# Token scales in two pieces, a gate's scaling behind the next low part, and more projection ahead of the second inverse

## The chip, the core and the metric

The kernel runs on one core of a Trainium2 chip. The metric is the device time of one execution in microseconds. Five engines matter here. TensorE (PE in the profile, PEld for its weight loads) multiplies, VectorE (DVE) and ScalarE (ACT) work elementwise and empty the accumulation banks, GpSimd (POOL) works elementwise between buffers of the on-chip memory, and SyncE (SP) issues the transfers.

## The reference, cut to what matters

One layer of a hybrid encoder over 16 meta tokens and 512 real ones, model width 2048:

```python
hn = rmsnorm(h_res, norm_in_g)
P = hn @ w_in                       # 2048 -> 8320 columns
# RWKV-7 half: token shift, then r, k, v, g (1024 wide each), low-rank inputs wl, al
decay = exp(-exp(-softplus(-(w0 + tanh(wl) @ w_lora_up)) - 0.5))
a = sigmoid(a0 + al @ a_lora_up)
kk = k * k_k / norm(k * k_k);  k = k * (1 + (a - 1) * k_a)
y = recurrence(r, decay, k, v, kk, kk * a)   # 16 heads of 64, delta rule
y_a = (groupnorm(y) + bonus) * silu(g)
# convolution half: B, C, h, g_c (1024 wide each)
y_b = B * causal_conv3(C * h) * silu(g_c)
h_res = h_res + concat(y_a, y_b) @ w_out
out = rmsnorm(h_res)[16:]
```

## The kernel before, in words

**Products.** Everything is kept transposed, channels on the partitions. The input projection is cut into 65 column tiles of 128 (`plan`: first the low-rank tile lora, then k0, r0, B0, v0, k1 and so on; k, r, v, g belong to the RWKV half, C, h, B, gc to the convolution half). Both operands are split into a high and a low part, and a product of a 128x128 block is three products: high by high, high by low x, low weight by high x (`steps`, line 328 is the matmul). A column tile with 528 or 514 tokens takes 96 matmuls in two banks, one with 512 tokens (B, gc) takes 48 in one bank.

**Weights.** `prefetch` (from line 138) issues one transfer of 128x1024 on SP and splits it into two quarters of 128x512: ACT casts the high part (line 134), DVE or POOL subtracts to get the low part (line 135). Six quarters fit (`slot`, six buffers). DVE makes the low part of the first quarter of each transfer, POOL that of the second. The dictionary `low` holds the low part's instruction of each quarter.

**Token scales.** The normalisation is not applied to the input. Its factor per token, `rs`, multiplies each projection as it leaves its bank (`scaled`, line 352). The factor is made once, in `token_scale_sums` and `token_scale`: five small matmuls sum the squares of 128 tokens each (line 459), DVE divides and adds (line 463), POOL raises the eight columns to the power -1/2 in one instruction (`rsqrt`, line 98) and copies five of them out to 128 columns each (`yb`, line 468). TensorE transposes each, so that the factor of a token lies on all partitions (lines 475 and 478), and DVE copies the result into `rs` (lines 476 and 479).

**The first four tiles.** lora, k0, r0 and B0 go side by side, a quarter of each at a time (`mains`). In the last round, the sums stand after k0, four transposes stand between r0's first bank and its second, the fifth stands in the middle of B0.

**Stages.** Pairs of heads are prepared two at a time (`prepare`), and `invert` inverts their triangular matrices together. The first call, for 0 and 1, is the first inverse; the call for 2 and 3 is the second. In `invert`, two 32x32-block transposes per pair member on DVE (`xn`, line 843) feed small matmuls on TensorE (`t`, line 852: 32 for the first member, then 32 for the second). Between such steps, `fill(ns)` lets projection matmuls through, each counted at 0.43 ns a column (220 ns for 512 columns), until the given time is used. `FW["solve_first"]` is 30,000 and `FW["solve"]` 24,500 for the later three. The projection's order does not change by that, only what stands between its matmuls. After an inverse, `prepare` asks for the next k tile to be complete (`until`).

**Order.** TensorE's order is written out by hand: it is the order of the program. The queues of DVE, ACT and POOL are put in an order by a planner that works with its own estimates of time; weights and some steps are given a higher priority. `issue_after(x)` adds that an instruction on x's engine stands behind x in that queue. `behind_of("split")` uses it: lines 521 and 522 store for B tiles 1 to 3 the first low part of the next tile, and `use` puts the scaling of the B tile behind it (line 436). For the gate tiles gc the scaling has no such tie. An engine's queue is worked off in order, so whatever stands ahead of an instruction has to be done first.

Of the kernel before, what the change touches and what calls it, by code (L numbers as in the profile page):

```python
# [18 lines left out]
P = 128  # L19
# [3 lines left out]
META = 16  # L23
# [54 lines left out]
def hymba_kernel(ctx: ExitStack, tc: tile.TileContext, xt, xtok, front, w_in, w_out, pv, lup, cst, msk, gf, out):  # L78
    nc = tc.nc
# [17 lines left out]
    def rsqrt(y, v):  # L97
        nc.gpsimd.tensor_tensor(out=y, in0=v, in1=mhalf[:, 0 : v.shape[1]], op=ALU.pow)
# [217 lines left out]
    REAL = ((0, SEQ),)  # L316
    PLACED = ((0, SEQ, META), (SEQ, SEQ + 2, META - 2), (SEQ + 2, L, 0))

    def steps(ps, ranges, k4, q, ks=range(4), rs_=range(2)):
        hi, lo = quarters[q]  # L320
        for r, (a, b) in enumerate(ranges):
            if r not in rs_:
                continue
            for k in ks:
                kt = 4 * k4 + k
                w = slice(k * P, (k + 1) * P)
                for n, (ww, xx) in enumerate(((hi, xh), (hi, xl), (lo, xh))):
                    nc.tensor.matmul(  # L328
                        ps[r], ww[:, w], xx[:, kt, a:b], start=(kt == 0 and n == 0), stop=(kt == KT - 1 and n == 2)
                    )  # L330
                    yield (b - a) * 0.43
# [14 lines left out]
    def scaled(ranges, ps, dst, base):  # L346
        for (a, b), p in zip(ranges, ps):
            for c, d, t in PLACED:
                c0, d0 = max(a, c), min(b, d)
                if c0 < d0:  # L350
                    o = t + c0 - c - base
                    nc.vector.tensor_tensor(
                        out=dst[:, o : o + d0 - c0], in0=p[:, c0 - a : d0 - a], in1=rs[:, c0:d0], op=ALU.mult
                    )
# [42 lines left out]
    def behind_of(what):  # L397
        return tc.issue_after(state.pop(what)) if what in state else nullcontext()

    def use(what, i, ps):  # L400
        if what == "lora":
            use_lora(ps)
        elif what in ("k", "v"):
            t = cq.tile([P, LP], F32, tag=what, name=f"{what}{i}")
            nc.gpsimd.memset(t[:, META:CH], 0.0)
            shift_full(ps, tile_of[what] + i, f"{what}{i}", padded(t))
            got[what, i] = t
        elif what in ("r", "g"):
            t = cq.tile([P, SEQ], F32, tag=f"r{i % 2}" if what == "r" else "g", name=f"{what}{i}")
            shift_real(ps, tile_of[what] + i, f"{what}{i}", t)  # L410
            if what == "g":
                gate(t, f"r{i}")
                later(14000, lambda: nc.sync.dma_start(gated[i], t))
            got[what, i] = t
        elif what == "C":
            u = tm(f"u{i}")
            scaled(TAIL, ps, u, 14)
            got[what, i] = u
        elif what == "h":
            u = got["C", i]  # L420
            hh = tm(f"hh{i}")
            with behind_of("turned"):
                scaled(TAIL, ps, hh, 14)
            n = SEQ + 2
            nc.gpsimd.tensor_tensor(out=u[:, 0:n], in0=u[:, 0:n], in1=hh[:, 0:n], op=ALU.mult)
            cv = tp.tile([P, SEQ], F32, tag="cw", name=f"cv{i}")
            nc.scalar.activation(cv, u[:, 0:SEQ], AF.Copy, scale=col(V_CW, i))
            for j in (1, 2):
                nc.vector.scalar_tensor_tensor(
                    out=cv, in0=u[:, j : j + SEQ], scalar=col(V_CW, 8 * j + i), in1=cv, op0=ALU.mult, op1=ALU.add  # L430
                )
            got[what, i] = cv
            if i == 0:
                nc.gpsimd.tensor_tensor(out=cv, in0=cv, in1=got["B", 0], op=ALU.mult)
        elif what == "B":
            b = tm(f"b{i}")[:, 0:SEQ] if i else cq.tile([P, SEQ], F32, name="b0")
            with behind_of("split"):
                scaled(REAL, ps, b, META)
            got[what, i] = b
            if i:  # L440
                nc.gpsimd.tensor_tensor(out=got["h", i], in0=got["h", i], in1=b, op=ALU.mult)
        else:
            cv = got["h", i]
            g = tm(f"gc{i}")[:, 0:SEQ]
            scaled(REAL, ps, g, META)
            gate(g, f"c{i}")
            o = direct.get(8 + i, cv)
            nc.vector.scalar_tensor_tensor(out=o, in0=cv, scalar=0.5, in1=g, op0=ALU.mult, op1=ALU.mult)
            if o is cv:
                later(9000, lambda: nc.sync.dma_start(mixd[8 + i], cv))  # L450
        ready.add((what, i))
# [4 lines left out]
    def token_scale_sums():  # L456
        pss = pi.tile([P, 8], F32, tag="misc", name="pss")
        for j, (a, b) in enumerate(((0, 128), (128, 256), (256, 384), (384, 512), (512, L))):
            nc.tensor.matmul(pss[0 : b - a, j : j + 1], accd[:, a:b], cs[:, C_ON : C_ON + 1], start=True, stop=True)
        var = tp.tile([P, 3, 8], F32, tag="nv", name="var0")  # L460
        nc.gpsimd.memset(var[:, 0], 1.0)
        for a, b, n in ((0, 4, P), (4, 5, META)):
            nc.vector.tensor_scalar(
                out=var[:n, 0, a:b], in0=pss[:n, a:b], scalar1=1.0 / DM, scalar2=RMS_EPS, op0=ALU.mult, op1=ALU.add
            )
        rsqrt(var[:, 1], var[:, 0])
        yb = cq.tile([P, 5, P], F32, tag="gt0", name="yb")
        nc.gpsimd.tensor_copy(yb, var[:, 1, 0:5].unsqueeze(2).to_broadcast([P, 5, P]))
        return yb

    def token_scale(yb, part):
        prs = pi.tile([P, 512], F32, tag="misc", name="prs")
        if part == 0:
            for j in range(4):
                nc.tensor.transpose(prs[:, j * P : (j + 1) * P], yb[:, j], ident)
            nc.vector.tensor_copy(rs[:, 0:512], prs)
        else:
            nc.tensor.transpose(prs[:, 0:META], yb[0:META, 4], ident[0:META, 0:META])
            nc.vector.tensor_copy(rs[:, 512:L], prs[:, 0:META])

    def mains():
        pa = banks(FULL, "lora", pm, "main")
        pb = banks(FULL, "k0", pz, "tz")
        pc = banks(TAIL, "r0", pm, "main")
        pd = [pi.tile([P, SEQ], F32, tag="ser", name="ps_B0")]
        four = ((pa, FULL), (pb, FULL), (pc, TAIL), (pd, REAL))
        for k in range(4):
            for n, (ps, rg) in enumerate(four):
                if k == n == 0:
                    hi, lo = quarters[0]  # L490
                    for ww, xx, first in ((hi, xh, True), (lo, xh, False), (hi, xl, False)):
                        for p, (a, b) in zip(ps, rg):
                            nc.tensor.matmul(p, ww[:, 0:P], xx[:, 0, a:b], start=first, stop=False)
                            yield (b - a) * 0.43
                    continue
                yield from steps(ps, rg, 0, 2 * n, (k,))
        for k4 in range(1, 4):
            for n, (ps, rg) in enumerate(four):
                h = 4 * (k4 // 2) + n
                if k4 == 2:  # L500
                    prefetch(h + 3)
                if (k4, n) == (3, 2):
                    yb = token_scale_sums()
                if (k4, n) == (3, 3):
                    yield from steps(ps, rg, k4, 2 * h + k4 % 2, range(2))
                    token_scale(yb, 4)
                    use("lora", 0, pa)
                    use("k", 0, pb)
                    yield from steps(ps, rg, k4, 2 * h + k4 % 2, range(2, 4))
                    continue  # L510
                for r in range(2 if n < 3 else 1):
                    if (k4, n, r) == (3, 2, 1):
                        token_scale(yb, 0)
                    yield from steps(ps, rg, k4, 2 * h + k4 % 2, range(4), (r,))
        use("r", 0, pc)
        use("B", 0, pd)
        for j in range(4, len(plan)):
            what, i = plan[j]
            rg = FULL if what in ("k", "v") else REAL if what in ("B", "gc") else TAIL
            ps = yield from main(j, rg, f"{what}{i}")  # L520
            if what == "B" and i < 4:
                state["split"] = low[4 * j + 4]
            use(what, i, ps)

# [305 lines left out]
    def invert(two):  # L830
        first = two[0]["i"]
        both = range(2)
        fill(FW["solve"] if first else FW["solve_first"])
        run_pending(float("inf"))


# [680 lines left out]
```

## Time and profile before

| what | value |
|---|---|
| median of 3 runs | 1017.98 us (1017.09 to 1019.04) |
| the profiled execution | 1016.83 us, its span 1015.1 us |
| granted TensorE clock over that span | 0.998 |
| PE busy | 995.6 us, 98% |
| DVE busy | 684.3 us, 67% |
| ACT busy | 393.9 us, 39% |
| POOL busy | 276.2 us, 27% |

A row of the timeline gives start and duration in us, the engine, the line of the kernel, the operation, the tiles written and read, their shapes and how many instructions were merged into the row; in brackets stands how long the engine was idle before it and what ended that. The list of waits has, for each instruction and releaser, the total in us, how often, and the longest.

### The profile page before, as it was taken

The numbers are of one execution on the slowest core, as the hardware profiler recorded it, in microseconds if no ns is written. First come the engines' busy times: TensorE is split into PE (matmuls) and PEld (weight loads), VectorE is DVE, ScalarE is ACT, GpSimd is POOL, SyncE is SP. The second block draws the span as 40 slices with busy tenths as digits, with TensorE's granted clock in tenths as the row PEclk, the third lists the DMA queues.
The fourth block names the chain that finished last, engine by engine and source line by source line (L and its number), as shares of the span: only waits on it lengthen the run. The fifth ranks groups of instructions, "written<-read, shape, count | busy, mean of one in ns | idle before, by whom it ended". The sixth has DMA issues, their size and how long they took to land.

```text
span 1015.1 us, 23761 instructions
## 1 busy us (share of the span) xinstructions
PE 995.6 (98%) x9723; PEld 913.6 (90%) x9723; DVE 684.3 (67%) x1305; ACT 393.9 (39%) x729; POOL 276.2 (27%) x292
## 2 busy tenths in 40 slices
PE   9999999999999999999999999999999999999996
PEld 8899998999988999998999998889898897787875
DVE  7677955587775568654668654244555697998787
ACT  7553423344323433323434323222222335545453
POOL 0122323233232323222423222223332332015001
PEclk9999999999999999999999999999999999999999
DMA  9525576446664363864273956977673698696754
GB/s 325 158 75 140 127 193 172 120 119 149 160 167 134 100 176 87 220 166 118 83 172 95 222 140 188 342 241 229 220 211 88 196 264 190 171 330 139 174 124 166
DMA packets 185037, 174.83 MB, mean 172 GB/s; under 512 B 121568, under 2 KB 142816, under 8 KB 184416
## 3 DMA queue, kind: packets, MB, share of 16 engines
q1 hardware_dynamic: 182336, 164.40, 56.3%
q0 software_dynamic: 2304, 8.39, 5.0%
q8 instruction: 76, 1.25, 0.5%
q10 hardware_dynamic: 288, 0.52, 0.1%
q14 instruction: 33, 0.27, 0.1%
HBM read 136.92 MB, written 36.35 MB: 171 GB/s over the span
## 4 chain that ended last, share of the span: by engine, by line
PE 55%; DVE 8%; DMA 3%; issue 2%; ACT 1%; SPq 0%; POOL 0%; DVEq 0%; ACTq 0%; POOLq 0%
PE ps_gc L328 8%; PE ps_B L328 7%; PE ps_h L328 7%; PE ps_C L328 6%; PE ps_v L328 5%; PE ps_k L328 5%; PE ps_g L328 4%; PE ps_r L328 4%; DVE o L1213 3%; DMA wo<-in_w_out_dram 2%; PE M L1240 2%; PE zy L1009 1%; PE zs L1005 1%; PE g L680 1%; DVE xb L1221 1%
## 5 line engine op out<-in xcount | busy, mean ns | idle before, releaser
L134 ACT CAST w<-wr 128x512 fp32r<-128x512 f32 x252 | 153.2, 618 | 292.7 <-PE ps_k L328 45.8
L135 POOL TENSOR_TENSOR w<-wr,w 128x512 fp32r<-128x512 f32 x119 | 166.6, 1400 | 362.0 <-ACT w L134 310.6
L135 DVE TENSOR_TENSOR w<-wr,w 128x512 fp32r<-128x512 f32 x133 | 94.3, 715 | 104.7 <-ACT w L134 99.6
L328 PE MATMUL ps_k<-xh,w 128*128 128x256 f32 (+1 forms) x512 | 95.6, 284 | 1.1 <-DVE w L135 1.1
L328 PE MATMUL ps_r<-xh,w 128*128 128x256 f32 (+1 forms) x512 | 95.7, 282 | 0.0
L328 PE MATMUL ps_v<-xh,w 128*128 128x272 f32 (+1 forms) x512 | 95.1, 283 | 0.0
L328 PE MATMUL ps_h<-xh,w 128*128 128x258 f32 (+1 forms) x512 | 94.1, 282 | 0.0
L328 PE MATMUL ps_C<-xh,w 128*128 128x258 f32 (+1 forms) x512 | 93.2, 281 | 0.0
L328 PE MATMUL ps_g<-xh,w 128*128 128x258 f32 (+1 forms) x512 | 92.2, 281 | 0.0
L328 PE MATMUL ps_B<-xh,w 128*128 128x512 f32 x256 | 83.4, 394 | 0.0
L328 PEld LDWEIGHTS ps_k<-xh,w 128*128 128x128 f32 x512 | 80.5, 190 | 1.6 <-DVE w L135 1.4
L328 PE MATMUL ps_gc<-xh,w 128*128 128x512 f32 x256 | 81.4, 393 | 0.3 <-DVE w L135 0.3
L328 PEld LDWEIGHTS ps_r<-xh,w 128*128 128x128 f32 x512 | 80.5, 189 | 0.2
L328 PEld LDWEIGHTS ps_h<-xh,w 128*128 128x128 f32 x512 | 79.7, 189 | 0.7
L328 PEld LDWEIGHTS ps_v<-xh,w 128*128 128x128 f32 x512 | 80.1, 189 | 0.3
L328 PEld LDWEIGHTS ps_C<-xh,w 128*128 128x128 f32 x512 | 79.6, 189 | 0.6
L328 PEld LDWEIGHTS ps_g<-xh,w 128*128 128x128 f32 x512 | 79.4, 189 | 0.5
L328 PE MATMUL ps_k<-xl,w 128*128 128x272 f32 (+1 forms) x256 | 73.1, 286 | 0.0
L328 PE MATMUL ps_h<-xl,w 128*128 128x256 f32 (+1 forms) x256 | 72.0, 281 | 0.6 <-issue 0.6
L328 PE MATMUL ps_v<-xl,w 128*128 128x256 f32 (+1 forms) x256 | 72.5, 283 | 0.0
L328 PE MATMUL ps_r<-xl,w 128*128 128x256 f32 (+1 forms) x256 | 72.3, 282 | 0.0
L328 PE MATMUL ps_g<-xl,w 128*128 128x256 f32 (+1 forms) x256 | 72.2, 282 | 0.0
(321 smaller groups left out, 2278.0 us busy)
## 6 DMA issues: line engine op xcount, KB each, us to landing
wr<-in_w_in_dram SPq DMA_DIRECT2D x126, 512.0 KB
ct<-opd SPq DMA_DIRECT2D x64, 288.0 KB
wo<-in_w_out_dram SPq DMA_DIRECT2D x24, 512.0 KB
x<-in_w_out_dram POOLq DMA_DIRECT2D x16, 512.0 KB, 6.2
opd<-ar SPq DMA_DIRECT2D x8, 576.0 KB
opd<-gt SPq DMA_DIRECT2D x16, 288.0 KB
opd<-bt SPq DMA_DIRECT2D x64, 64.0 KB
x<-in_w_out_dram SPq DMA_DIRECT2D x8, 512.0 KB
```

What stands on the lines that cost most here:

```text
L134: nc.scalar.copy(hi, rq)
L135: low[q] = eng.tensor_tensor(out=lo, in0=rq, in1=hi.bitcast(F32), op=ALU.subtract).ins
L328: nc.tensor.matmul(ps[r], ww[:, w], xx[:, kt, a:b], start=(kt == 0 and n == 0), stop=(kt == KT - 1 and n == 2))
L680: nc.tensor.matmul(z[h][:, c - c0], bk[hs, c, h : h + 2, :].rearrange("p a s -> p (a s)"), ar[hs, c].rearrange("p a s -> p (a s)"), start= ...
L1005: nc.tensor.matmul(d[hs, j], w, x[hs], start=(a == 0), stop=(a == b - 1))
L1009: nc.tensor.matmul(d[ho, j], t[hs, o : o + CH], x[hs], start=(a == 0), stop=(a == b - 1))
L1213: nc.vector.tensor_tensor(out=lo, in0=rq, in1=hi.bitcast(F32), op=ALU.subtract)
L1221: nc.vector.tensor_tensor(out=h, in0=h, in1=ps, op=op)
L1240: nc.tensor.matmul(bank[s], left(prod, jj, m, s), w, start=(jj == 0 and n == 0), stop=(jj == 7 and n == 2))
```

## The change

Four edits in three places.

- The power is taken in two instructions, columns 0 to 3 and then column 4, each followed by its own copy into `yb`. Before, it was one power over eight columns and one copy of five.
- The four transposes are moved from between r0's two banks to behind r0's second bank, ahead of B0's last quarter. The fifth stays in the middle of that quarter.
- The scaling of gate tile gc0 is tied behind the first low part of the tile that follows it (k2).
- `fill` ahead of the second inverse gets 2,400 ns more, 26,900 in place of 24,500. The other inverses keep theirs.

```diff
         else:
             cv = got["h", i]
             g = tm(f"gc{i}")[:, 0:SEQ]
-            scaled(REAL, ps, g, META)
+            with behind_of("split"):
+                scaled(REAL, ps, g, META)
             gate(g, f"c{i}")
...
-        rsqrt(var[:, 1], var[:, 0])
         yb = cq.tile([P, 5, P], F32, tag="gt0", name="yb")
-        nc.gpsimd.tensor_copy(yb, var[:, 1, 0:5].unsqueeze(2).to_broadcast([P, 5, P]))
+        for a, b in ((0, 4), (4, 5)):
+            rsqrt(var[:, 1, a:b], var[:, 0, a:b])
+            nc.gpsimd.tensor_copy(yb[:, a:b], var[:, 1, a:b].unsqueeze(2).to_broadcast([P, b - a, P]))
         return yb
...
                 if (k4, n) == (3, 3):
+                    token_scale(yb, 0)
                     yield from steps(ps, rg, k4, 2 * h + k4 % 2, range(2))
                     token_scale(yb, 4)
...
                 for r in range(2 if n < 3 else 1):
-                    if (k4, n, r) == (3, 2, 1):
-                        token_scale(yb, 0)
                     yield from steps(ps, rg, k4, 2 * h + k4 % 2, range(4), (r,))
...
-            if what == "B" and i < 4:
+            if what == "B" and i < 4 or (what, i) == ("gc", 0):
                 state["split"] = low[4 * j + 4]
...
-        fill(FW["solve"] if first else FW["solve_first"])
+        fill(FW["solve"] + 2400 * (first == 2) if first else FW["solve_first"])
```

## The prediction

> **What bounds the kernel now.** I read the page first, then TensorE's waits over the whole span, then the timeline at each wait.
>
> ```profile
> span 1015.1 us, 23761 instructions
> PE 995.6 (98%) x9723; PEld 913.6 (90%) x9723; DVE 684.3 (67%) x1305; ACT 393.9 (39%) x729; POOL 276.2 (27%) x292
> ```
> ```profile
> PE t L852 <- DVE xn L843: 2.0, 1, 2.0
> PE prs L475 <- POOL yb L468: 1.7, 1, 1.7
> ...
> PE ps_k L328 <- DVE w L135: 1.1, 1, 1.1
> ```
>
> TensorE is busy 98% of the span, so until its projection is used up the time is its work plus its waits. Three waits carry this case: for `yb`, for a low weight part ahead of k2, for a block transpose in the second inverse. The change adds no TensorE work, so it can win about 4.8 us at most, and each part has to be asked what is late next.
>
> **Part 1, token scales.**
>
> ```profile
> 47.81 1.98 POOL L98 TENSOR_TENSOR var<-var,mhalf 128x8 f32<-128x8 f32 x1 [0.28 <-DVE var L463]
> 49.85 0.72 POOL L468 COPY yb<-var 128x640 f32<-128x640 f32 x1
> 48.64 0.28 PE L328 MATMUL ps_r<-xh,w 128*128 128x256 f32 x1
> 50.62 0.66 PE L475 MATMUL prs<-cs,yb 128*128 128x128 f32 x4 [1.71 <-POOL yb L468]
> 51.04 0.36 PE L328 MATMUL ps_r<-xh,w 128*128 128x258 f32 x1
> 52.57 0.39 PE L328 MATMUL ps_B<-xh,w 128*128 128x512 f32 x1
> 51.32 0.69 DVE L476 COPY rs<-prs 128x512 f32<-128x512 f32 x1 [3.06 <-PE prs L475]
> 52.04 0.76 DVE L352 TENSOR_TENSOR pr_lora<-ps_lora,rs 128x256 f32<-128x256 f32 x2
> 54.05 0.23 PE L478 MATMUL prs<-cs,yb 16*128 16x16 f32 x1
> 54.53 0.24 DVE L352 TENSOR_TENSOR pr_lora<-ps_lora,rs 128x2 f32<-128x2 f32 x2
> 59.10 0.10 POOL L358 MEMSET pr_v<- 128x1 f32 x1 [8.38 <-DVE k L363]
> ```
> ```profile
> L98 POOL TENSOR_TENSOR nv<-nv,mhalf x8: 1635/1637/1678, 671.3 to 786.2; 128x8 f32<-128x8 f32 x8
> L98 POOL TENSOR_TENSOR fv<-fv,mhalf x4: 547/572/857, 999.8 to 1008.8; 128x1 f32<-128x1 f32 x4
> ```
>
> When is the first `yb` ready? Between one column (0.572 us) and eight (1.637 us) a straight line gives 1.03 us for four; the first use here took 0.34 us more than the other eight-column ones, so 1.03 to 1.37 us. The copy of 512 of 640 columns is 0.8 x 0.72 = 0.57 us. With 0.06 us between them `yb` is there at 49.5 to 49.8 us. The second bank of r0 took 52.57 - 51.04 = 1.53 us; it now starts about 48.8 and ends at 50.3. The transposes wait for nothing: 1.71 us won. If the power did not shrink with its columns, `yb` came at 50.4 and 0.1 us would be lost.
>
> What is late next: the fifth transpose. It now comes 0.42 us (50.62 to 51.04) of transposes and 1.48 us (52.57 to 54.05) of B0 after 50.3, at 52.2. Its own power and copy (0.57 to 0.86 us, and some 0.2 us for a fifth of the old copy's columns) end by 51.0; the two instructions that POOL issues more stand in front of 8.38 us of idle time (59.10). It writes the same bank as the four, so the copy into `rs` must be over: 0.70 us (50.62 to 51.32) after the transposes begin, plus 0.69, is 51.7. If the planner puts a low part (0.69 us) ahead of that copy, it ends at 52.5 and 0.4 us is lost. I take 1.7 us, with 1.3 and 1.85 as ends (1.85 if refilling the pipeline after the idle time is saved too).
>
> The evacuation of lora and k0 gains only 0.3 us while TensorE gains 1.7. Who notices?
>
> ```profile
> 55.72 0.28 PE L328 MATMUL ps_v<-xh,w 128*128 128x256 f32 x1
> 59.01 0.70 DVE L393 TENSOR_TENSOR la<-lora_th,la 64x528 fp32r<-64x528 f32 x1
> 61.69 0.29 PE L570 MATMUL tz<-la,luh 128*128 128x272 f32 x1
> ```
>
> v0 takes lora's first bank at 54.0; that bank is read right after `rs` (52.04, less 0.3). Its second bank is due some 1.5 us later, as r0's was, at 55.5, and lora's last pieces (before 54.77) are read by 54.5. The low-rank product comes at 60.0 and needs `la`, ready at 59.71 - 0.3 = 59.4. Both hold, the second by 0.6 us. Beyond that, each later step is set off by TensorE and moves with it.
>
> **Part 2, the gate's scaling.**
>
> ```profile
> 159.98 2.17 ACT L134 CAST w<-wr 128x512 fp32r<-128x512 f32 x4
> 167.62 0.69 DVE L352 TENSOR_TENSOR gc<-ps_gc,rs 128x512 f32<-128x512 f32 x1 [5.38 <-PE ps_gc L328]
> 168.23 0.68 DVE L135 TENSOR_TENSOR w<-wr,w 128x512 fp32r<-128x512 f32 x1
> 168.97 0.53 PE L328 MATMUL ps_k<-xh,w 128*128 128x272 f32 x2 [1.13 <-DVE w L135]
> 170.17 1.82 DVE L448 SCALAR_TENSOR_TENSOR cv<-cv,gc 128x512 f32<-128x512 f32 x1 [0.46 <-DVE gc L382]
> 171.91 2.37 DVE L135 TENSOR_TENSOR w<-wr,w 128x512 fp32r<-128x512 f32 x2
> 170.14 1.29 POOL L135 TENSOR_TENSOR w<-wr,w 128x512 fp32r<-128x512 f32 x1 [4.25 <-issue]
> 174.20 0.70 DVE L843 STREAM_TRANSPOSE xn<-xT 128x512 f32<-128x512 f32 x1
> 174.85 1.16 PE L852 MATMUL t<-xn,gt 64*64 64x64 f32 x64
> ```
>
> VectorE stood idle for 5.38 us behind a scaling that waited for TensorE, with the low part queued after it; its cast was over by 162.15. Ahead of the scaling, the low part runs in that idle time and the 1.13 us wait goes. Late next is the first inverse: the second member's 32 products start in the middle of the 64, about 175.36 (in the second inverse 32 such take 0.69 us with the last one's tail), and its transpose ended at 174.90. With TensorE 1.13 us ahead, they are due at 174.23, and the transpose still hangs on the gate (scaling, tanh, `cv`, two low parts), which starts when gc0's products end. That gives a new wait of 0.7 us. Net 0.4 us; the ends are 0 (the transpose slips further) and 1.13 (the planner moves it up, or `cv` is quick).
>
> Why `cv` is slow matters here: 1.82 us, beginning just after POOL's low part at 170.14, where the six of its kind have a median of 0.69 us.
>
> ```profile
> L448 DVE SCALAR_TENSOR_TENSOR cv<-cv,gc x6: 686/693/1818, 170.2 to 747.4; 128x512 f32<-128x512 f32 x6
> ```
> [...]
>
> **Part 3, the second inverse.**
>
> ```profile
> 301.00 3.45 DVE L135 TENSOR_TENSOR w<-wr,w 128x512 fp32r<-128x512 f32 x2
> 304.37 0.70 DVE L843 STREAM_TRANSPOSE xn<-xT 128x512 f32<-128x512 f32 x1
> 302.46 0.69 PE L852 MATMUL t<-xn,gt 64*64 64x64 f32 x32
> 305.13 0.69 PE L852 MATMUL t<-xn,gt 64*64 64x64 f32 x32 [1.97 <-DVE xn L843]
> 307.48 0.69 DVE L135 TENSOR_TENSOR w<-wr,w 128x512 fp32r<-128x512 f32 x1 [2.41 <-ACT w L134]
> ```
> ```profile
> 791.78 10.88 PE ps_gc L328 x48
> ```
>
> 2,400 ns at 220 ns a product lets 11 more products through, at 10.88 / 48 = 0.227 us each 2.5 us. The first 32 then start at 304.96, the second 32 at 305.47; the transpose ends at 305.07. The 1.97 us wait goes with 0.4 us to spare, if VectorE's order stays. The 11 products are taken from what followed, so they cost nothing, and the loads and stores that are timed by counted projection keep their distance from it; B1 and gc1 only end earlier against the inverse, and the next stage falls back into step when it asks for k4. The ends are 0 and 2.0; I take 2.0, since the row needs only TensorE to arrive later.
>
> **The sum.** 1.7 + 0.4 + 2.0 = 4.1 us off the profiled execution's 1016.83 gives 1012.7. The median shown, 1017.98, is 1.15 us above it; against it the forecast is 1013.9 us, 0.40% faster. The three runs lie within 1.95 us, so 0.2% (2.0 us) is about what can be told from no change.
>
> **Rivals.**
>
> *Part of it is given back* (0.18). One of the two large waits stays or comes back elsewhere: `la` has 0.6 us to spare, the second transpose 0.4. For it: VectorE's order comes from a planner, and both margins are short. Against: elsewhere every wait moves with TensorE. 4.1 less 1.7 or 2.0 leaves 2.1 to 2.4 us: 1015.6 to 1015.9; with part 2 at nothing too, 1016.3.
>
> *The change does nothing* (0.08). The stalls only move: low parts ahead of `rs`, of `la` and of both transposes. For it: in row 301.00 that has happened already. 1017.0 to 1018.5.
>
> *The second inverse gets worse* (0.14), the one on the other side. With B1 further on when the inverse comes, the planner may put the next low part (307.48) ahead of the transpose, and that one waits for its cast.
>
> ```profile
> 144.80 1.14 ACT L134 CAST w<-wr 128x512 fp32r<-128x512 f32 x2 [4.84 <-DMA wr<-in_w_in_dram]
> ```
>
> With that low part at its old time the transpose ends at 308.9, 3.4 us after it is due: the 2.0 gained turn into 1.4 lost, and 0.7 us stay of the sum. If its transfer is late too, as the cast at 144.80 shows (4.84 us), the loss is some 6 us and the time 1020.1 or more. It decides from a transpose that ends after 311.6. Against it: the transpose ended 2.41 us before that low part had its cast, so the planner's order would have to change, not only its times.
>
> [...]
>
> **How the numbers follow.** Forecast 0.60 (1012.5 to 1015.0, by the ends of its terms and 0.5 us of scatter), given back 0.18, nothing 0.08, worse 0.14. Faster by over 0.2% means below 1015.9: the forecast and some half of the second case, 0.70. Slower means above 1020.0: most of the last, 0.13. The rest, 0.17, lies between. The range 1011.9 to 1018.0 leaves out the last case and a little below: 0.2.
>
> **What would show it.** TensorE's waits without `yb` and without `ps_k`; four transposes just ahead of B0's last quarter; a short wait of `t` in the first inverse and none in the second. It is wrong if `t` or `tz` waits over 1 us, if `la` comes after the low-rank product is due, or if a new wait for a low part appears behind any of the three places.

## The result, and the profile after

The changed kernel takes 1012.65 us (median of 6 runs, 1011.91 to 1013.78). The kernel before takes 1018.81 us (6 runs, the three shown above among them, 1017.09 to 1019.79). The ratio is 0.995, 95% interval 0.994 to 0.9961: 0.4 to 0.6% faster. The profiled execution took 1012.36 us against 1016.83.

First the head of the page and TensorE's waits (releaser: total us, times, longest), of the changed kernel. All lines behind the edits have moved down by one.

```profile
span 1010.6 us, 23763 instructions
PE 995.3 (98%) x9723; PEld 913.0 (90%) x9723; DVE 684.2 (68%) x1305; ACT 393.8 (39%) x729; POOL 276.8 (27%) x294
```
```profile
PE M L1241 <- DVE o L1214: 1.5, 4, 0.7
...
PE t L853 <- DVE xn L844: 0.8, 1, 0.8
PE ps_h L328 <- issue: 0.7, 1, 0.7
```

The work is the same (995.3 us of TensorE, 995.6 before). The waits for `yb` (1.7) and for k2's low part (1.1) have left the list. The wait of `t` for `xn` fell from 2.0 to 0.8 us, and it is not the same wait: it now stands in the first inverse, where there was none.

Since TensorE's order is written by hand, the start of one and the same product in both traces tells how much was saved up to there. TensorE's timeline before, and then after, at the five sums, at v0, k3 and k5 (before's row of v0, 55.72, stands in the prediction):

```profile
46.26 0.39 PE L459 MATMUL pss<-cs,accd 128*128 128x1 f32 x3
208.68 0.29 PE L328 MATMUL ps_k<-xh,w 128*128 128x272 f32 x1
362.79 0.29 PE L328 MATMUL ps_k<-xh,w 128*128 128x272 f32 x1
```
```profile
45.89 0.28 PE L460 MATMUL pss<-cs,accd 128*128 128x1 f32 x2
53.75 0.28 PE L328 MATMUL ps_v<-xh,w 128*128 128x256 f32 x1
206.47 0.29 PE L328 MATMUL ps_k<-xh,w 128*128 128x272 f32 x1
358.74 0.29 PE L328 MATMUL ps_k<-xh,w 128*128 128x272 f32 x1
```

From sums to v0 it was 55.72 - 46.26 = 9.46 us and is 7.86 now: 1.6 us saved by part 1. From v0 to k3, with the first inverse inside, 152.96 became 152.72: 0.24 us for part 2. From k3 to k5, with the second inverse inside, 154.11 became 152.27: 1.84 us for part 3. Together 3.7 us. Of the 4.47 us between the two executions another 0.37 us was there at the sums already, ahead of the first edit, and 0.48 us came up between k5 and the output's first product, where nothing was changed. I use these three stretches as a ledger for all kernels below, always against the kernel before:

| kernel | sums to v0 | v0 to k3 | k3 to k5 | sum |
|---|---|---|---|---|
| after | 1.61 | 0.24 | 1.84 | 3.69 |
| after again (e12) | 1.61 | 0.24 | 1.88 | 3.72 |
| part 1 alone (e1) | 1.61 | 0.01 | -1.61 | 0.01 |
| part 2 alone (e2) | 0.01 | 0.23 | -1.53 | -1.29 |
| part 3 alone (e3) | 0.00 | -0.03 | 1.87 | 1.85 |
| e4 | 1.62 | 1.00 | 1.96 | 4.57 |
| e5 | 1.46 | 0.22 | 1.85 | 3.52 |
| e6 | 0.37 | 0.18 | 1.87 | 2.42 |
| e7 | 1.61 | 1.18 | 1.88 | 4.67 |
| e8 | 1.59 | 0.26 | 1.14 | 2.99 |
| e9 | 1.62 | 0.17 | 1.83 | 3.61 |
| e10 | 1.80 | 1.17 | 2.05 | 5.01 |
| e11 | 1.61 | 0.19 | 1.96 | 3.75 |

A stretch with the same edit in it, or with none, repeats within some 0.1 us (e10's last stretch within 0.2), with two exceptions: e1 and e2 lose over 1.5 us in a stretch that neither edits. What happened there is told with them. The ledger is of one profiled execution each and leaves out what lies ahead of the sums and behind k5, where executions differ by up to 1 us.

The three places in the timeline of after. Part 1:

```profile
47.33 1.99 POOL L98 TENSOR_TENSOR var<-var,mhalf 128x4 f32<-128x4 f32 x2 [0.16 <-DVE var L464]
49.27 0.85 POOL L470 COPY yb<-var 128x512 f32<-128x512 f32 x2
49.94 0.42 PEld L477 LDWEIGHTS prs<-cs,yb 128*128 128x128 f32 x4 [0.15 <-POOL yb L470]
50.68 0.69 DVE L135 TENSOR_TENSOR w<-wr,w 128x512 fp32r<-128x512 f32 x1 [2.79 <-ACT w L134]
51.29 0.68 DVE L478 COPY rs<-prs 128x512 f32<-128x512 f32 x1
52.09 0.13 PEld L480 LDWEIGHTS prs<-cs,yb 16*128 16x128 f32 x1 [0.54 <-issue]
```

The transposes start at 49.94, where only the weight load still waits 0.15 us for `yb`. POOL did not work power, copy, power, copy: both powers come first (x2: 1.47 us for four columns and 0.55 for one, 1.99 us together, as long as the old single one with its 1.98), then both copies. And a low part (50.68) did run ahead of the copy into `rs`.

Part 2, the first inverse, and part 3, the second:

```profile
159.60 2.37 DVE L135 TENSOR_TENSOR w<-wr,w 128x512 fp32r<-128x512 f32 x2
165.76 0.69 DVE L352 TENSOR_TENSOR gc<-ps_gc,rs 128x512 f32<-128x512 f32 x1 [3.78 <-PE ps_gc L328]
168.28 1.30 POOL L135 TENSOR_TENSOR w<-wr,w 128x512 fp32r<-128x512 f32 x1 [3.90 <-issue]
168.31 1.81 DVE L449 SCALAR_TENSOR_TENSOR cv<-cv,gc 128x512 f32<-128x512 f32 x1 [0.46 <-DVE gc L382]
170.04 2.37 DVE L135 TENSOR_TENSOR w<-wr,w 128x512 fp32r<-128x512 f32 x2
172.34 0.70 DVE L844 STREAM_TRANSPOSE xn<-xT 128x512 f32<-128x512 f32 x1
173.09 0.69 PE L853 MATMUL t<-xn,gt 64*64 64x64 f32 x32 [0.79 <-DVE xn L844]
```
```profile
302.19 0.70 DVE L844 STREAM_TRANSPOSE xn<-xT 128x512 f32<-128x512 f32 x1
303.16 1.16 PE L853 MATMUL t<-xn,gt 64*64 64x64 f32 x64
```

The low part now runs in VectorE's idle time, two of them in the row at 159.60, and k2 waits for nothing. Behind the gate the chain is as slow as it was (`cv` 1.81 us), so the second transpose comes 0.79 us late for TensorE. In the second inverse the 64 products are one block.

### The profile page after: what moved, and what is told of

Same layout as the page of the kernel before. It is cut to its first block, busy times and chain, and to the rows that moved or that the text cites. A ratio compares the mean times of both kernels' runs of the same rounds, so it can differ in the third digit from the quotient of the medians.

```text
span 1010.6 us, 23763 instructions
## 1 busy us (share of the span) xinstructions
PE 995.3 (98%) x9723; PEld 913.0 (90%) x9723; DVE 684.2 (68%) x1305; ACT 393.8 (39%) x729; POOL 276.8 (27%) x294
## 3 DMA queue, kind: packets, MB, share of 16 engines
q8 instruction: 76, 1.25, 0.5%
## 4 chain that ended last, share of the span: by engine, by line
PE 56%; DVE 8%; DMA 3%; issue 2%; ACT 1%; POOL 0%; DVEq 0%; ACTq 0%; SPq 0%; POOLq 0%
PE ps_gc L328 8%; PE ps_B L328 7%; PE ps_h L328 7%; PE ps_C L328 7%; PE ps_k L328 5%; PE ps_v L328 5%; PE ps_g L328 5%; PE ps_r L328 5%; DVE o L1214 3%; DMA wo<-in_w_out_dram 2%; PE M L1241 2%; PE zy L1010 1%; PE zs L1006 1%; PE g L681 1%; DVE xb L1222 1%
## 5 line engine op out<-in xcount | busy, mean ns | idle before, releaser
L328 PE MATMUL ps_C<-xl,w 128*128 128x256 f32 (+1 forms) x256 | 71.9, 281 | 0.0
```

What stands on the lines that cost most here:

```text
L328: nc.tensor.matmul(ps[r], ww[:, w], xx[:, kt, a:b], start=(kt == 0 and n == 0), stop=(kt == KT - 1 and n == 2))
```

## The experiments

### Each part alone

My theory was that the parts are three separate waits, so that each brings its term alone. The rival was that one part's gain only feeds the next wait. The diffs of e1 to e3 are against the kernel before, all later ones against after.

*e1, part 1 alone.*

```diff
-        rsqrt(var[:, 1], var[:, 0])
         yb = cq.tile([P, 5, P], F32, tag="gt0", name="yb")
-        nc.gpsimd.tensor_copy(yb, ...)
+        for a, b in ((0, 4), (4, 5)):
+            rsqrt(var[:, 1, a:b], var[:, 0, a:b])
+            nc.gpsimd.tensor_copy(yb[:, a:b], ...)
...
+                    token_scale(yb, 0)      # ahead of B0's last quarter
...
-                    if (k4, n, r) == (3, 2, 1):
-                        token_scale(yb, 0)
```

> Token scales alone (power and copy in two pieces, transposes behind r0); the gate's scaling and the second inverse as before. If the three waits are independent, TensorE reaches v0 1.6 us earlier than before, the wait for yb is gone, the waits of 1.1 us (k2) and 2.0 us (second inverse) stand as before, and the time is 1.6 us under the kernel before. If instead a gain made at 50 us is eaten by later waits that hang on transfers, k2 or the second inverse would wait longer than before by what was won, and the time would be within 0.5 us of before.

*e2, part 2 alone.*

```diff
-            scaled(REAL, ps, g, META)
+            with behind_of("split"):
+                scaled(REAL, ps, g, META)
...
-            if what == "B" and i < 4:
+            if what == "B" and i < 4 or (what, i) == ("gc", 0):
```

> The gate's scaling tied behind k2's first low part, alone. By the forecast's term the wait of k2 (1.13 us) goes and a wait of 0.7 to 0.8 us appears in the first inverse, where the second member's transpose still hangs on the gate: net 0.3 to 0.4 us under before. If the new wait comes from the token scales' gain (TensorE ahead of VectorE by 1.6 us) and not from this edit, the first inverse does not wait here and the gain is 1.1 us.

*e3, part 3 alone.*

```diff
-        fill(FW["solve"] if first else FW["solve_first"])
+        fill(FW["solve"] + 2400 * (first == 2) if first else FW["solve_first"])
```

> 2,400 ns more projection ahead of the second inverse, alone. If the 11 products are free, the wait of 1.97 us goes, nothing new appears, and the time is 1.8 to 2.0 us under before, all of it gone by k5. If the products are missed later, a wait shows up behind the second inverse (in k4 or before k5) and the gain is under 1 us.

Beside a median of 1016.99 us of the kernel before, e1 took 1015.3 us (ratio 0.9984, 0.9974 to 0.9993), e2 1018.23 us (1.001, 1.000 to 1.002) and e3 1015.1 us (0.9982, 0.9974 to 0.9991). In the ledger each part brings in its own stretch what it brings in after: 1.61, 0.23 and 1.87 us. So they are separate, and no part lives on another's wait.

But e1 and e2 lose 1.61 and 1.53 us between k3 and k5, where they are the same program as before. The windows (length, then busy us of PE, PEld, DVE, ACT and POOL, then the granted clock, the DMA share and GB/s) around the second inverse, two in a row each, of e1:

```profile
299.81:303.22 3.41, 1.44 (x57) 0.95 (x59) 3.00 (x3) 0.00 (x0) 2.08 (x3) 1.00 0.41 129
303.22:306.63 3.41, 3.41 (x31) 2.71 (x24) 0.69 (x1) 2.11 (x4) 0.63 (x1) 0.50 0.67 219
```

and of the kernel before, and of e2:

```profile
300.56:303.97 3.41, 2.60 (x41) 1.87 (x39) 3.41 (x3) 1.02 (x2) 3.30 (x3) 1.00 0.45 150
303.97:307.39 3.42, 2.26 (x39) 1.94 (x40) 1.10 (x2) 1.54 (x4) 0.18 (x1) 1.00 0.78 234
```
```profile
301.54:304.95 3.41, 1.44 (x38) 0.91 (x36) 3.35 (x3) 0.00 (x0) 2.42 (x3) 1.00 0.44 108
304.95:308.37 3.42, 3.42 (x38) 2.82 (x39) 0.64 (x1) 2.11 (x4) 0.02 (x1) 0.50 0.72 237
```

In each, the products of the second inverse wait 1.97 us for the transpose (of before, row 305.13 in the prediction; here of e1 and of e2):

```profile
302.87 0.88 PE L852 MATMUL t<-xn,gt 64*64 64x64 f32 x32 [1.97 <-DVE xn L843]
```
```profile
304.94 1.13 PE L853 MATMUL t<-xn,gt 64*64 64x64 f32 x32 [1.97 <-DVE xn L844]
```

Before, the clock stays at 1.00. In e1 it falls to one half for 3.41 us from 303.2, right behind the wait; in e2 from 305.0. Half of 3.41 us is 1.7 us lost, which is the ledger's 1.5 to 1.6. So these two profiled executions were held up by the clock and not by the edits. How often a low clock occurs, and what differs in the profile of before, is told below, with the hardware.

Here the clock decides how the medians are read. They do not add up: 1.69 and 1.89 us won and 1.24 lost make 2.3, and after again (e12, below) wins 4.9 beside its own run of before. The ledger's parts do: 1.61, 0.23 and 1.87 make 3.71, beside 3.69 for after. With a mean clock of 0.996 or below were 10 of 27 executions of before, 4 of 11 of e1, 6 of 11 of e2 and 1 of 11 of e3. Held against executions of before at the same mean clock, 0.996 or below and then 0.998, e1 is 1.9 and 1.6 us shorter (1016.78 and 1014.97 against 1018.71 and 1016.52). e2's six executions at 0.996 or below are level with those of before (1018.67), but its five at 0.997 or 0.998 have a median of 1017.40, 0.9 us above the 1016.51 of 17 such of before. So more executions at a low clock are one part of e2's 1.2 us and the rest is open; part 2 alone shows no gain in these times, only its 0.23 us in the ledger.

### Part 1: what of it brings the time?

*e5: one power and one copy as before, with the transposes moved.*

```diff
-        for a, b in ((0, 4), (4, 5)):
-            rsqrt(var[:, 1, a:b], var[:, 0, a:b])
-            nc.gpsimd.tensor_copy(yb[:, a:b], ...)
+        rsqrt(var[:, 1], var[:, 0])
+        nc.gpsimd.tensor_copy(yb, ...)
```

> The changed kernel with one power over eight columns and one copy of five, as before, but the transposes behind r0. Power 1.98 and copy 0.72 us: yb comes some 0.15 us after TensorE is through r0's second bank, as in the changed kernel, where the power over column 4 turned out to run before the first copy (1.99 us for both). If moving the transposes is what matters, the time is within 0.3 us of the changed kernel. If the pieces matter, TensorE waits 0.5 us or more for yb and the time is that much above.

*e6: two powers and two copies, with the transposes at their old place.*

```diff
-                    token_scale(yb, 0)      # ahead of B0's last quarter
...
+                    if (k4, n, r) == (3, 2, 1):
+                        token_scale(yb, 0)
```

> The changed kernel with the transposes back between r0's two banks, power and copy in two pieces. If moving the transposes is what matters, TensorE waits about 1.6 us for yb there (0.1 us less than before at most, since the copy is smaller) and the time is 1.5 us above the changed kernel. If the pieces bring it, the wait is under 1 us.

Beside 1017.26 us of before, e5 took 1013.97 us (0.9964, 0.9952 to 0.9976) and e6 1014.7 us (0.9969, 0.996 to 0.9979). The four transposes in the timeline of e5 and of e6:

```profile
50.53 0.66 PE L476 MATMUL prs<-cs,yb 128*128 128x128 f32 x4 [0.27 <-POOL yb L469]
```
```profile
50.22 0.66 PE L477 MATMUL prs<-cs,yb 128*128 128x128 f32 x4 [1.38 <-POOL yb L470]
```

The move alone saves 1.46 us of the 1.61, the pieces alone 0.37. With the move, what is left of the wait is 0.27 us, and that is all the pieces still have to take away. On POOL the pieces bring the first copy's end 0.33 us closer to the sums (3.98 us behind them in e6, 4.31 before), in three equal steps of 0.11: the power starts sooner, the copy starts sooner after the power began, and it takes 0.61 us in place of 0.72. The smaller first power itself brings nothing forward, since the second one is taken ahead of the first copy.

### Part 2: what holds the second transpose?

The prediction named a new wait of 0.7 us in the first inverse and put it down to the late gate and a slow `cv` (1.82 us, begun just after POOL's low part at 170.14). If that is so, and if POOL is what makes `cv` slow, which nothing had shown by then, two quite different edits remove it: more projection ahead of the first inverse (TensorE arrives later), or POOL kept away from VectorE while `cv` runs (the transpose is earlier).

*e4: after, with 1,000 ns more ahead of the first inverse.*

```diff
-        fill(... if first else FW["solve_first"])
+        fill(... if first else FW["solve_first"] + 1000)
```

> The changed kernel with 1,000 ns more projection ahead of the first inverse too (31,000 in place of 30,000): nine products of k2, about 1.05 us. If the wait of 0.79 us in the first inverse is what the gate's part gives back, it goes and the time is 0.8 us under the changed kernel (5.3 us under before). If VectorE's queue moves with the products, so that the transpose slips by as much, the wait stays and the time is that of the changed kernel.

*e7: after, with POOL's low parts of transfers 27 and 28 on VectorE.*

```diff
-                    split_w(..., nc.gpsimd if q and 10 < j < N_IN else nc.vector)
+                    split_w(..., nc.gpsimd if q and 10 < j < N_IN and j not in (27, 28) else nc.vector)
```

> The changed kernel with two low parts (second quarters of transfers 27 and 28) made by VectorE in place of POOL, so that POOL runs nothing beside the gate's cv and the low parts behind it in the first inverse. If POOL's low parts are what makes cv take 1.8 us and the next low part 1.77, both fall to 0.69, the transpose comes 0.3 to 1.0 us earlier in spite of two more low parts ahead of it, and the wait of 0.79 us in the first inverse shrinks below 0.4. If cv is slow by itself, the transpose comes 1.4 us later and the wait grows to 2 us.

e4 took 1012.94 us beside 1016.99 (0.9961, 0.9947 to 0.9975), e7 1013.35 us beside 1017.26 (0.9961, 0.9946 to 0.9975). Against after's 0.995 neither is to be told apart. The traces tell more. The products of e4, and then `cv`, the low parts, the transpose and the products of e7:

```profile
172.53 1.16 PE L853 MATMUL t<-xn,gt 64*64 64x64 f32 x64
```
```profile
168.77 0.69 DVE L449 SCALAR_TENSOR_TENSOR cv<-cv,gc 128x512 f32<-128x512 f32 x1 [0.47 <-DVE gc L382]
169.37 2.49 DVE L135 TENSOR_TENSOR w<-wr,w 128x512 fp32r<-128x512 f32 x4
171.78 0.71 DVE L844 STREAM_TRANSPOSE xn<-xT 128x512 f32<-128x512 f32 x1
172.06 1.17 PE L853 MATMUL t<-xn,gt 64*64 64x64 f32 x64
```

Both have the 64 products in one block and no wait, and gain 0.76 and 0.94 us in that stretch over after. In e7 `cv` falls from 1.81 to 0.69 us, and four low parts on VectorE take 2.49 us where two took 2.37 beside POOL. So POOL's low part was what slowed VectorE, and the late gate together with that slowness was the new wait. The 0.47 us of idle time ahead of `cv` stayed (0.46 in after); its cause is open.

### Part 3: how far can the second inverse be moved?

The prediction gave the second transpose 0.4 us to spare, and its rival on the other side said that with B1 further on the planner may put the next low part ahead of it.

*e8 and e9: after, with 1,200 and with 7,200 ns more in place of 2,400.*

```diff
-        fill(FW["solve"] + 2400 * (first == 2) if first else FW["solve_first"])
+        fill(FW["solve"] + 1200 * (first == 2) if first else FW["solve_first"])
```

> The changed kernel with 1,200 ns in place of 2,400 ahead of the second inverse: six products (1.36 us). If the wait simply shrinks by what TensorE comes later, 1.97 - 1.36 = 0.6 us of it is left in the second inverse, and the profile's span is 0.6 us above the changed kernel's. If the order of VectorE's queue decides, the wait is either 2 us or none.

> The changed kernel with 7,200 ns in place of 2,400: 33 products, so that B1 is over and gc1 ten products in when the second inverse begins. VectorE's queue has B1's scaling ahead of the second transpose then. If projection ahead of the inverse is free however much it is, no wait in the second inverse and the same span within 0.3 us. If moving more of it brings another step ahead of the transpose that costs, as the rival on the other side had it, the second inverse waits again, by 0.5 us or more.

One execution each: e8 1012.96 us, e9 1012.24 us, beside 1016.61 of before. The products of e8, and VectorE and the products of e9:

```profile
302.93 0.69 PE L853 MATMUL t<-xn,gt 64*64 64x64 f32 x32 [0.48 <-DVE xn L844]
```
```profile
305.41 0.69 DVE L352 TENSOR_TENSOR b<-ps_B,rs 128x512 f32<-128x512 f32 x1 [3.73 <-PE ps_B L328]
306.02 0.70 DVE L844 STREAM_TRANSPOSE xn<-xT 128x512 f32<-128x512 f32 x1
307.57 1.16 PE L853 MATMUL t<-xn,gt 64*64 64x64 f32 x64
```

Half the step leaves 0.48 us of the wait and saves 1.14 us in place of 1.84: TensorE's arrival sets the wait. Three times the step does bring other work ahead of the transpose (B1's scaling, which waits for B1's own products), but TensorE comes as much later, and the products wait for nothing. The rival had named the next low part and not this scaling, and the price is nil over the range tried.

*e11: after, with 2,400 ns less than before (22,100), meant to make the wait long, 4.4 us, and so to see whether the clock falls more often behind a longer wait; e12: after again beside it, on the same chip.*

```diff
-        fill(FW["solve"] + 2400 * (first == 2) if first else FW["solve_first"])
+        fill(FW["solve"] - 2400 * (first == 2) if first else FW["solve_first"])
```

> The changed kernel with 2,400 ns less than before, 4,800 less than in the change, ahead of the second inverse (22,100). TensorE comes 2.5 us earlier than in the kernel before, so it waits some 4.4 us there. If a wait of this length only costs itself, the time is 4.4 us above the changed kernel and the granted clock of its runs is that of the changed kernel (0.997 to 0.998). If such a wait makes the granted clock fall for one window of 3.41 us, as the profiles of two kernels with a 2.0 us wait show (at 303.2 and 305.0 us, at half the clock), nearly every run has it, with 0.996 or less, and the time is about 6 us above the changed kernel.

> The changed kernel once more, beside the longer wait on the same chip. No wait over 1 us is left in its first 330 us, so if the clock falls because of waits, its runs stay at 0.997 to 0.998 and lie within 2 us of each other, while a good part of the runs of the kernel before are at 0.996 or less and some 2 us above its other runs. If the falls have another cause, both kernels show them equally often.

Beside 1017.99 us of before, e11 took 1013.43 us (0.9949, 0.9935 to 0.9962), e12 1013.08 us (0.9948, 0.9936 to 0.9961). What was expected of e11 did not come. The second inverse in its timeline:

```profile
298.07 0.71 DVE L844 STREAM_TRANSPOSE xn<-xT 128x512 f32<-128x512 f32 x1 [4.45 <-DMA xT<-sx]
298.13 1.40 PE L853 MATMUL t<-xn,gt 64*64 64x64 f32 x64
298.70 0.78 DVE L352 TENSOR_TENSOR hh<-ps_h,rs 128x256 f32<-128x256 f32 x3
301.67 1.54 DVE L429 SCALAR_TENSOR_TENSOR cv<-u,pvt,cv 128x512 f32<-128x512 f32 x2 [2.18 <-ACT cv L427]
```

With less projection the planner put the second transpose too ahead of `hh`, the convolution step and the low parts, so the products found both ready. Less projection removes the wait as well as more does (1.96 against 1.84 and 1.88 us in the ledger). So the 2 us of before came of an order of VectorE with low parts between the two transposes. That order stands at 24,500 ns, in e8 and in after alike; in the last two TensorE only comes later to it. The test of the clock, for which e11 was made, did not take place. What was expected of e12 did come: its five executions were at 0.997 or 0.998 and within 1.4 us of each other, while 6 of 9 of before were at 0.996 or 0.995.

One rival stands untested here. The two low parts ahead of the transpose took 3.45 us together in the kernel before (row 301.00), beside two on POOL; the four of e7 without POOL took 2.49. At e7's pace the transpose would have come some 2.2 us sooner (an estimate, 3.45 less half of 2.49), and by that the wait would have been gone with the order unchanged. No run takes POOL away at this place.

### The pieces put together

*e10: after, with e4's 1,000 ns, and the fifth transpose one block of B0 later.*

```diff
                     token_scale(yb, 0)
-                    yield from steps(ps, rg, k4, 2 * h + k4 % 2, range(2))
+                    yield from steps(ps, rg, k4, 2 * h + k4 % 2, range(3))
                     token_scale(yb, 4)
...
-        fill(... if first else FW["solve_first"])
+        fill(... if first else FW["solve_first"] + 1000)
```

> The changed kernel with 1,000 ns more projection ahead of the first inverse, and the fifth transpose one block of B0 later (three matmuls, 0.68 us). In the changed kernel VectorE made a low part ahead of the copy into rs, and TensorE reached the fifth transpose's bank 0.3 us early. With both edits: 0.8 + 0.3 = 1.1 us under the changed kernel, 5.6 us under before. If the idle time at the fifth transpose is only the switch to another kind of matmul, the second edit brings nothing and it is 0.8 us.

e10 took 1012.12 us beside 1017.26 (0.9947, 0.9934 to 0.996). The fifth transpose in its timeline:

```profile
52.77 0.13 PEld L480 LDWEIGHTS prs<-cs,yb 16*128 16x128 f32 x1 [0.35 <-issue]
```

The idle time ahead of it fell from 0.54 to 0.35 us and the first stretch gained 0.2 us over after, which is what the low part ahead of `rs` had cost; 0.37 us stand there in before too (at 54.05), where no low part is ahead of `rs`. The ledger gives e10 1.3 us more than after, the most of all kernels, and its profiled execution is the shortest (1011.32 us). The measured ratios, 0.9947 and 0.995, do not separate the two.

## Why the prediction was right, and where not

The forecast of 1013.9 us lies 1.25 us above the measured 1012.65, inside its range, and the sign is right. Its terms:

- **Part 1** was taken at 1.7 us with ends 1.3 and 1.85, and brought 1.61 (eight kernels between 1.59 and 1.62). The 0.14 us of the upper end, for refilling the pipeline, no run shows. The mechanism held with two differences. "1.03 to 1.37 us" for the first power was too short and wrong in its order: four columns took 1.47 us, and POOL took both powers first. Counted from the sums, `yb` was there after 4.0 us (49.27 + 0.62 - 45.89) and not after 3.2 to 3.5 (49.5 and 49.8 less 46.26). It did little harm because r0's second bank covered all but 0.15 us of it. And the case that the prediction named but did not take, a low part ahead of the copy into `rs`, did occur; it cost 0.2 us, if what e10 won back is its price, where 0.4 were reckoned. That the move carries the part and the pieces hardly matter (e5, e6) was in its numbers, "if the power did not shrink ... 0.1 us would be lost" (measured 0.15), but was not drawn out. The low-rank product came with `la` ready, as it said: it starts at 59.74, and `la` of 58.04 ends at 58.74.
- **Part 2** was taken at 0.4 us, 1.13 less a new wait of 0.7. The wait measured 0.79, the gain 0.24; 1.13 less 0.79 would be 0.34, and the last 0.1 us is not accounted for. e4 and e7 show that this wait and the 1.81 us `cv` are what kept the rest: with either removed the stretch gains 1.0 to 1.18 us, close to the upper end of the term, 1.13.
- **Part 3** was taken at 2.0 us and brought 1.84. The 11 products cost nothing and the transposes keep ahead of TensorE. The reason "the row needs only TensorE to arrive later" was half of it. e8 supports it, but e11 shows that VectorE's order made the wait, and not the amount of projection as such: an earlier inverse loses it too.
- **The sum** of 4.1 us for the profiled execution compares with 3.7 in the ledger and 4.47 between the executions. 0.37 us of the 4.47 were there ahead of the first edit.
- **The step from profile to median** is the term that was mis-sized: "1.15 us above it" was carried over unchanged from before to after. After's median lies only 0.29 us above its profile. The reason that fits is the clock: the kernel before is often at a mean of 0.996 or below (22 of the 53 executions counted below), and its profiled execution, at 0.998, was not; e1 and e2 lost 1.61 and 1.53 us at half the clock behind the second inverse's wait, and with the wait gone 2 of 57 executions are at 0.996 or below. This makes up 0.86 us of the 1.25 us by which the forecast was too high. It is argued, not shown: for the six executions behind 1018.81 us no clock is on record.

Of the rivals, "part of it is given back" did not come: nothing of the 1.6 and 1.8 us returned elsewhere in the trace. "The change does nothing" named low parts ahead of `rs`, `la` and the transposes; the first occurred, at 0.2 us. "The second inverse gets worse" came near in e9, with B1's scaling in place of the low part and without a price. Its sum was off by its own terms: 1.7 and 0.4 us won and "some 6 us" lost give 1021.9 us and not 1020.1.

## What to carry to other kernels

Where a wait is a matter of when one engine's queue gets to an instruction, look for what to set between the two before making anything faster: 1.46 of part 1's 1.61 us came from moving four transposes behind work that was ready, and 0.15 from the smaller pieces. Of each removed wait ask which one comes due next and price it from the trace; here that gave 0.7 against a measured 0.79 us. And when one program's executions differ by more than the edit is worth, hold the same instructions of two traces against each other, stretch by stretch, and look at the granted clock in each.

## What the runs showed of the hardware

**A 2 us wait can cost 3.5.** The granted clock fell to one half for one stretch of 3.41 us in e1 (303.22 to 306.63) and in e2 (304.95 to 308.37), right behind the 1.97 us wait of the second inverse, with small 64x64 products around it; 1.61 and 1.53 us were lost there in the ledger. In the kernel before the same wait of 1.97 us was followed by no fall. What differs in the windows shown with e1 and e2 is how the wait lies in them. In e1 and in e2 the 3.41 us ahead of the fall hold the whole wait, and TensorE is busy for 1.44 us of them. In the traces of before and after the full clock is recorded for 1003.52 and 1000.11 us, which is 294 and 293 times 3.413 us. With before's trace cut into such stretches, a border at 303.97 divides the wait, TensorE is busy for 2.60 and 2.26 us, and the clock stays full. Of all such stretches of before and after, up to where TensorE runs out of work, the one with the least has 1.70 us (before, from 47.99, with the 1.71 us wait for `yb` in it), and the clock stays full behind it too. The last one of each, with none, is followed by half the clock to the end of the span (from 1010.55 and 1006.31).

That the place of the wait between such borders decides is my reading of these profiles, not shown: no run moves the one against the other. If it does, a wait of 1.97 us lies whole in a stretch of 3.41 in 42% of all positions (an estimate, 1.44 of 3.41). Each execution comes with its mean granted clock over the span, in which 1.7 us of 1015 lost is a fall from 0.998 to 0.996 (an estimate, half of 3.41 us over the span). The last 4.5 us of before's span and 4.3 us of after's, where TensorE has run out of work, are at half the clock as well; their means are 0.998, those of e1 and e2, with the fall, 0.996. Of the eleven other profiles e5's shows 0.996, the rest 0.997 or 0.998. Of the kernels that hold this wait (before 53 executions, without the single one beside e8 and e9, e1 11, e2 11) 32 of 75 were at 0.996 or below, 43%; of those that do not (after, e3 to e7, e10 to e12) 2 of 57. By chip it is 26 of 58 against 1 of 26 on one and 6 of 17 against 1 of 25 on another (after's first six, with none, aside), so the chip is not the cause. Of the two, one is e5's profile; the other, of e3, took 1014.47 us, less than e3's median, so not every low mean is time lost.

The kernel before took 1016.7 us in the median of its 23 executions at 0.998 and 1018.8 us in the 22 at 0.996 or below. Its median differs from one set of executions to the next as the share of low means does: 1016.99 us with 10 of 27, 1017.26 with 6 of 17, 1017.99 with 6 of 9. The executions are a count beside a reading and not an experiment on it: the run that was to lengthen the wait had none. e6 kept a 1.38 us wait for `yb`, and none of its 10 executions was at 0.996 or below.

**A low part on POOL slows VectorE, and the other way round.** Two low parts on VectorE take 2.37 us beside POOL's, four take 2.49 us without; `cv` takes 1.81 us beside it and 0.69 us without. In the kernel before the slow `cv` only stood beside POOL's low part (1.82 us at 170.17); e7 shows the cause by removal. POOL's side shows in the second inverse of before, where its two low parts beside VectorE's take 3.23 us together (1.56 and 1.71 us); a single one took 1.28 us at 134.41, with VectorE idle, and 1.29 us at 170.14, where it was `cv` that was slow.

```profile
300.67 3.23 POOL L135 TENSOR_TENSOR w<-wr,w 128x512 fp32r<-128x512 f32 x2 [1.92 <-ACT w L134]
```
